# A seven-product output projection in another block order, and a seam issued from one table of steps

## The chip, the cores and the metric

The program runs on one core of one Trainium2 chip. The metric is the device time of one execution in microseconds (us). The core has TensorE (PE, matrix products into PSUM), VectorE (DVE), ScalarE (ACT), GpSimd (POOL) and SyncE (SP, whose queue issues most DMAs). Each engine works through its own queue in order; semaphores tie the queues together.

## The reference, cut to what matters

One layer of a hybrid decoder on 1024 rows of width 1024 in float32. Two attention mixers are gated, added and projected; then comes a gated feed-forward block of inner width 2816 (`D_FF`).

```python
y = jax.nn.sigmoid(g_a) * (o_a @ w_o_swa[l]) + jax.nn.sigmoid(g_b) * (o_b @ w_o_mla[l])
x = x + y @ w_out[l]
h = rmsnorm(x, ffn_norm_g[l])
x = x + (jax.nn.silu(h @ w_gate[l]) * (h @ w_up[l])) @ w_down[l]
return rmsnorm(x, final_norm_g)
```

## The kernel before, in words

**Precision.** A float32 operand is used as a high and a low part. `split(hi, lo, src)` (L160, L161) lets ACT round the source into `hi`, and VectorE, or another engine if named, forms `lo = src - hi`. `mm3` (L167 to L169) multiplies with three matmuls: high by high, high by low, low by high.

**Seven products.** The large matrix products are cut into 2 x 2 blocks and formed from seven block products in place of eight, at the price of sums of blocks. Block products are numbered q = 1 to 7. Products 1, 2, 5 and 3 accumulate in PSUM bank group "A" (product 5 starts a new accumulation) and 6, 7 and 4 in group "B". `class Seven` does this for the gates and for the feed-forward: for each pair j of weight column blocks and each matrix m (gate "g", up "u"), `mix` forms sums of weight blocks on GpSimd, `prep` splits the weights of the next product, and `run` issues its 12 matmuls and what takes its result. Before product q = 7 `prep` also corrects one weight block on GpSimd (L172, `wr<-wr,sm`). In a raw weight tile the two column blocks of a pair lie in turn, so one block is four runs of 128 elements.

**Output projection.** x + y @ w_out runs as seven products of four row tiles t each, in the order `X_ORDER = (1, 2, 6, 7, 5, 4, 3)`. One step (q, t) is 12 matmuls into a PSUM tile `xo`; `xo_done` then adds or subtracts that tile on VectorE in one to three half rows of x2, the eight row tiles of the new x. Row tiles 0 to 3 are complete with the sixth product (q = 4), row tiles 4 to 7 with the seventh (q = 3). A list `prep` of 30 splits of y and w_out is worked off between the steps.

**The seam.** Each complete row tile b goes through `row_sum` (sum of squares on ACT, two small GpSimd operations), `row_norm` (one VectorE operation giving `xn`, and the store of x2 to DRAM), eight 128x128 transposes on TensorE into two PSUM tiles `tp` (`to_ps`), and `to_h`. For b below 4 `to_h` splits them as blocks b11 and b21 and keeps a copy `hraw`. For b from 4 it forms the block sums: t2 and t3 with b22 at once, t1 and t4 from what remains in `hraw`, split last by `late_split`. GpSimd does three subtractions per row tile there: `hraw - t`, the low part of t3 and the low part of t4. Feed-forward product 1 needs b11, 2 needs b21, 6 needs t2, 7 needs t3, 5 needs t1, 4 needs t4 and 3 needs b22. The feed-forward starts with products 1 and 2 of pairs 0 and 1 (`head`), eight runs that need row tiles 0 to 3 only, and then does 6, 7, 5, 4, 3 of pair 0, and of pair 1.

**Order.** Between `in_order.__enter__()` and its exit the queues of PE, DVE, ACT and POOL hold the instructions in the order in which the program issues them; elsewhere a planner orders them. Before, this stretch begins with the sixth product. After it, `ffn.run` prepares four runs ahead. `act_out` and `wd_out` prepare the operands of the down projection for each pair j: `wd_out` loads two tiles of w_down, subtracts blocks on GpSimd four times and stores the tiles to `rb_d`. It stands at q = 5 of pairs 0 and 1 and at q = 2 of the later ones; that of the last pair stands at q = 4 of pair 3.

**Buffers.** Tiles of 4 KB per partition come from 21 slots (`U`), tiles of 8 KB from 17 slots (`V`), PSUM tiles from two groups of four banks (`P1`, `PX`).

## Time and profile before

| | |
|---|---|
| median of 3 runs | 1364.37 us (1363.83 to 1364.56) |
| the profiled execution's own time | 1360.19 us |
| its span, first to last instruction | 1358.4 us |
| PE busy / weight loads busy | 1331.8 us / 1112.0 us |
| DVE / ACT / POOL busy | 944.6 / 653.4 / 596.2 us |
| granted TensorE clock | 0.999 |

Rows of groups read: line, engine, operation, out<-in, shapes, count, then busy time in all, mean ns of one, and idle time before them with what ended it. Rows of windows read: stretch, length, busy time and count of PE, weight loads, DVE, ACT, POOL (engines without work left out), then granted clock, DMA share and GB/s. Rows of waits read: who waited, on whom, us in total, times, longest. A busy PE is not PE at its peak, so counts of matmuls per window tell more than its busy time.

### The profile page before, as it was taken

Reading aid. Unit: us, or ns where it says so; the run is one execution under the profiler, and the core shown is the slowest. Engines: PE = TensorE matmul, PEld = TensorE weight load, DVE = VectorE, ACT = ScalarE, POOL = GpSimd, SP = SyncE. Lnnn points to the kernel's source line nnn. Section 1 sums busy time; section 2 is a strip of 40 time slices with the busy share of each in tenths; the row PEclk is TensorE's granted clock in tenths of the full one; section 3 lists DMA queues with packets and bytes.
Section 4 is the critical chain, followed back from the end, with each engine's and each line's share of the span. In section 5 each row is a group of like instructions: output and inputs, shape, how many; then the busy total and the mean of one; then the engine's idle time right before and its main releaser. Section 6 shows DMA issues by size and latency. Waiting matters only on the chain.

```text
span 1358.4 us, 18967 instructions
## 1 busy us (share of the span) xinstructions
PE 1331.8 (98%) x6552; PEld 1112.0 (82%) x6552; DVE 944.6 (70%) x1527; ACT 653.4 (48%) x1317; POOL 596.2 (44%) x636
## 2 busy tenths in 40 slices
PE   9999999999999999999999999999999999999997
PEld 6899878878788888888887788888888888888886
DVE  6868767776777887489878866666656664664862
ACT  7433667665567777654357232322332332644452
POOL 1115545553066555131045875766665541022521
PEclk9999999999999999999999999999999999999999
DMA  9454332335100111598041353645444425996503
GB/s 360 161 182 154 115 106 82 98 121 174 71 2 13 43 32 32 219 307 264 31 171 62 112 188 140 227 178 178 147 153 165 163 85 184 379 385 237 171 16 140
DMA packets 78239, 205.39 MB, mean 151 GB/s; under 512 B 8768, under 2 KB 15424, under 8 KB 77504
## 3 DMA queue, kind: packets, MB, share of 16 engines
q1 hardware_dynamic: 76848, 199.99, 41.5%
...
## 4 chain that ended last, share of the span: by engine, by line
PE 72%; DVE 7%; ACT 4%; issue 3%; POOL 3%; DMA 0%; POOLq 0%; ACTq 0%; DVEq 0%
PE fa L169 7%; PE fa L167 7%; PE fa L168 7%; PE fd L168 5%; PE fd L167 5%; PE fd L169 5%; PE fb L167 5%; PE fb L169 5%; PE fb L168 5%; DVE wl L161 2%; PE pTb L1161 2%; PE xo L167 1%; PE xo L168 1%; PE xo L169 1%; PE oA L167 1%
## 5 line engine op out<-in xcount | busy, mean ns | idle before, releaser
L161 DVE TENSOR_TENSOR wl<-wr,wl 128x512 fp32r<-128x512 f32 x150 | 154.6, 1052 | 75.4 <-ACT wl L160 75.1
L161 DVE TENSOR_TENSOR lrv<-lr,lrv 128x1024 fp32r<-128x1024 f32 x77 | 105.0, 1396 | 49.7 <-ACT lrv L160 47.1
L160 ACT CAST lrv<-lr 128x1024 fp32r<-128x1024 f32 x77 | 80.1, 1052 | 96.3 <-PE fd L169 56.0
L169 PE MATMUL fd<-lrv 128*128 128x512 f32 x308 | 119.9, 389 | 0.0
L168 PE MATMUL fd<-lrv 128*128 128x512 f32 x308 | 119.9, 389 | 0.0
L167 PE MATMUL fd<-lrv 128*128 128x512 f32 x308 | 119.9, 389 | 0.0
L172 POOL TENSOR_TENSOR wr<-wr,sm 128x512 f32<-128x512 f32 (+1 forms) x38 | 46.8, 1241 | 121.2 <-DVE wl L161 115.1
L160 ACT CAST wl<-wr 128x512 fp32r<-128x512 f32 x150 | 87.3, 623 | 3.1 <-DVE wr L816 2.6
L161 DVE TENSOR_TENSOR wl<-sm,wl 128x512 fp32r<-128x512 f32 x60 | 55.2, 946 | 45.4 <-ACT wl L160 45.4
L295 POOL TENSOR_SCALAR ms<-ss 128x1 f32<-128x1 f32 x32 | 9.8, 305 | 140.4 <-ACT xn L1582 62.5
L1146 POOL TENSOR_TENSOR denb<-denb,neg_one 128x1 f32<-128x1 f32 x64 | 36.4, 570 | 75.0 <-ACT p L1145 64.3
L167 PEld LDWEIGHTS fd<-lrv 128*128 128x128 f32 x308 | 57.8, 188 | 12.1
L169 PEld LDWEIGHTS fd<-lrv 128*128 128x128 f32 x308 | 57.8, 188 | 12.0
L168 PEld LDWEIGHTS fd<-lrv 128*128 128x128 f32 x308 | 57.8, 188 | 11.9
L1145 ACT ACTIVATE p<-scb,nmb 128x384 f32<-128x384 f32 (+3 forms) x64 | 47.5, 743 | 36.8 <-DVE nmb L1144 35.0
L161 DVE TENSOR_TENSOR ptl<-pTb,pth 128x512 fp32r<-128x512 f32 (+2 forms) x96 | 50.0, 549 | 13.6 <-ACT pth L160 12.8
L1144 DVE CUSTOM_DVE_ANT_0 scb<-scb,mask 128x384 f32<-128x384 f32 (+3 forms) x64 | 48.5, 758 | 14.1 <-PE scb L1136 13.7
L1485 ACT ACTIVATE act<-sm 128x512 f32<-128x512 f32 x11 | 7.0, 633 | 103.7 <-DVE sm L175 103.7
L1147 POOL TENSOR_SCALAR p<-p,denb 128x384 f32<-128x384 f32 (+3 forms) x64 | 49.1, 768 | 6.3
L1485 ACT ACTIVATE act<-pu 128x512 f32<-128x512 f32 x22 | 13.9, 632 | 74.8 <-DVE pu L175 74.8
L160 ACT CAST pth<-pTb 128x512 fp32r<-128x512 f32 (+2 forms) x96 | 42.9, 482 | 13.5 <-PE pTb L1161 12.9
L169 PE MATMUL fa<-t1h,wl 128*128 128x512 f32 x120 | 46.8, 391 | 2.6 <-DVE wl L161 2.6
...
## 6 DMA issues: line engine op xcount, KB each, us to landing
...
wr<-in_w_gate_dram SPq DMA_DIRECT2D x22, 512.0 KB, 4.3
wr<-in_w_up_dram SPq DMA_DIRECT2D x22, 512.0 KB, 5.0
wd<-in_w_down_dram SPq DMA_DIRECT2D x22, 512.0 KB, 6.4
rb_d<-wd SPq DMA_DIRECT2D x22, 512.0 KB, 2.6
la_d<-sd SPq DMA_DIRECT2D x22, 512.0 KB, 4.8
...
```

Source lines behind the costliest of these rows:

```text
L160: nc.scalar.copy(hi, src)
L161: (eng or nc.vector).tensor_tensor(lo, src, hi.bitcast(F32), op=ALU.subtract)
L167: nc.tensor.matmul(ps, ah, bh, start=first and i == 0, stop=False, skip_group_check=go_on)
L168: nc.tensor.matmul(ps, ah, bl, start=False, stop=False, skip_group_check=go_on)
L169: nc.tensor.matmul(ps, al, bh, start=False, stop=last and i == n - 1, skip_group_check=go_on)
L172: eng.tensor_tensor(out, a, b, op=ALU.subtract)
L1144: nc.vector.tensor_tensor_reduce(s_, s_, m_, 1.0, -NEG, op0=ALU.add, op1=ALU.min, accum_out=nm)
L1145: nc.scalar.activation(p_, s_, AF.Exp, scale=-1.0, bias=nm, accum_out=den)
L1146: nc.gpsimd.tensor_tensor(den, den, neg_one[:, 0:1], op=ALU.pow)
L1147: nc.gpsimd.tensor_scalar(p[:, 0:w], p[:, 0:w], den, 0.0, op0=ALU.mult, op1=ALU.add)
L1161: nc.tensor.transpose(pp[:, i], p[:, blk(k0 + i)], ident)
L1485: nc.scalar.activation(dst, src, AF.Silu)
```

## The change

- The output projection runs in the order (1, 2, 6, 5, 3, 7, 4), and the two halves of the rows change roles in it (`y_split`, `y_sums`, `xo_done`). Row tiles 0 to 3 are now complete with the fifth product (q = 3), row tiles 4 to 7 with the seventh (q = 4). Bank group "A" comes from `PX` and "B" from `P1`, the reverse of before.
- The stretch in program order begins with the fifth product, and everything in it is issued from the string `SEAM`, one token for a step: `x` an output projection step, `y` a split from `prep`, `s` and `n` row sum and norm, `T` transposes, `h`, `c` splits and copy of a row tile below 4, `a b 0 2 l 3 i e g F H` single operations of a row tile from 4, `t` and `v` the splits of t1 and t4, `m` and `M` the weight sums of pairs 0 and 1, `p` one prepared weight, `f` one feed-forward product, `D` the new DMA sums.
- The subtractions `i`, `H` and the low part of `v`, which GpSimd did, stand on VectorE. Signs are turned in several places (`plus`, scale -1).
- For pair 0 the correction before q = 7 is left out of `prep`; two accumulating DMAs issued by GpSimd (`mix_sum`, step 2) do it.
- `wd_out` of pairs 0 and 1 moves to q = 5 of pairs 2 and 3.
- A raw weight tile holds each column block of a pair in one run of 512 elements.
- `mix_load` and the other steps of `mix_sum` are defined and not called.

```diff
+                op = add if self.plus else sub
                 for k in range(0, 4, n):
                     k = slice(k, k + n)
                     add(s[:, 0, k], a21[:, k], a22[:, k], eng_)
-                    sub(s[:, 1, k], s[:, 0, k], a11[:, k], eng_)
-                    sub(a21[:, k], a11[:, k], a21[:, k], eng_)
+                    op(s[:, 1, k], s[:, 0, k], a11[:, k], eng_)
+                    op(a21[:, k], a11[:, k], a21[:, k], eng_)
...
+        def mix_sum(self, j, step):
+
+            def plus(dst, src):
+                nc.gpsimd.dma_start(dst, src, accum_op=ALU.add)
+
+            for m in self.ms:
+                a11, a22 = self.src[m][j, 0][:, 0], self.src[m][j, 1][:, 1]
+                s = self.sums[(j, m)]
+                if step == 0:
+                    for i in range(2):
+                        plus(s[:, i], a22)
+                elif step == 1:
+                    plus(s[:, 1], a11)
+                    plus(self.part(j, m, 0, 1), a11)
+                else:
+                    plus(self.part(j, m, 1, 0), s[:, 1])
...
-            if q == 7:
+            if q == 7 and j not in self.by_dma:
                 a12, s1 = self.part(j, m, 1, 0), self.sums[(j, m)][:, 1]
                 for k in range(0, 4, self.piece):
                     k = slice(k, k + self.piece)
-                    sub(a12[:, k], a12[:, k], s1[:, k], nc.gpsimd)
+                    (add if self.plus else sub)(a12[:, k], a12[:, k], s1[:, k], nc.gpsimd)
...
-                add(u2, ps, p1, nc.vector)
+                add(u2, ps, p1, nc.vector) if not self.plus else sub(u2, p1, ps, nc.vector)
             elif q == 7:
-                add(u3, ps, p1, nc.vector)
+                (sub if self.plus else add)(u3, ps, p1, nc.vector)
...
-        t = U("wr", F32, (P, 4, 2, P))
+        t = U("wr", F32, (P, 2, 4, P))
...
         if j == 0:
-            nc.vector.tensor_scalar(t[:, k], t[:, k], g, None, op0=ALU.mult)
+            nc.vector.tensor_scalar(t[:, :, k], t[:, :, k], g, None, op0=ALU.mult)
         else:
-            nc.scalar.activation(t[:, k], t[:, k], AF.Copy, scale=g)
+            nc.scalar.activation(t[:, :, k], t[:, :, k], AF.Copy, scale=g)
...
-        for sh in (1, 0):
...
-        src = y_new[0][:, k] if q == 5 else y[k + 4 * (q in (2, 3, 4))][:, half({1: 1, 2: 1, 6: 1, 7: 0, 4: 0, 3: 1}[q])]
+        src = y_new[0][:, k] if q == 5 else y[k + 4 * (q in (2, 3, 4))][:, half({1: 0, 2: 0, 6: 0, 7: 1, 4: 1, 3: 0}[q])]
...
-        a21, a11, a22, a12 = y[k][:, half(0)], y[k][:, half(1)], y[4 + k][:, half(0)], y[4 + k][:, half(1)]
+        a21, a11, a22, a12 = y[k][:, half(1)], y[k][:, half(0)], y[4 + k][:, half(1)], y[4 + k][:, half(0)]
...
-    def to_h(pss, b):
+    tps = {}
+
+    def seam_step(what, b):
 
         c = b % 4
-        if b < 4:
-            if b == 0:
-                new_h("b11")
-                new_h("b21")
-            raw1[b] = U("hraw", F32, (P, 2, 4, P))
+        pss = tps.get(b)
+        if what == "T":
+            tps[b] = to_ps(xn_of.pop(b))
+            if b in (0, 4):
+                for name in ("b11", "b21") if b == 0 else ("b22", "t2", "t3"):
+                    new_h(name)
+        elif what == "h":
             for kh in range(2):
                 split_h(("b11", "b21")[kh], c, pss[kh])
+        elif what == "c":
+            raw1[c] = U("hraw", F32, (P, 2, 4, P))
             for kh in range(2):
-                nc.scalar.copy(raw1[b][:, kh], pss[kh])
-            return
-        if b == 4:
-            for name in ("b22", "t2", "t3"):
+                nc.scalar.copy(raw1[c][:, kh], pss[kh])
+        elif what == "a":
+            t23[c] = U("t23", F32, (P, 2, 4, P))
+            nc.scalar.copy(t23[c][:, 1], pss[0])
+        elif what == "b":
+            nc.scalar.copy(hq["b22"][0][:, :, blk(c)], pss[1])
+        elif what == "0":
+            sub(raw1[c][:, 0], raw1[c][:, 0], pss[0], nc.vector)
+        elif what == "2":
+            nc.vector.scalar_tensor_tensor(t23[c][:, 0], pss[1], -1.0, raw1[c][:, 0], op0=ALU.mult, op1=ALU.subtract)
+        elif what == "l":
+            sub(hq["b22"][1][:, :, blk(c)], pss[1], hq["b22"][0][:, :, blk(c)].bitcast(F32), nc.vector)
+        elif what == "3":
+            sub(t23[c][:, 1], t23[c][:, 1], pss[1], nc.vector)
+        elif what == "i":
+            add(raw1[c][:, 1], raw1[c][:, 1], t23[c][:, 0], nc.vector)
+        elif what == "e":
+            nc.scalar.activation(hq["t2"][0][:, :, blk(c)], t23[c][:, 0], AF.Copy, scale=-1.0)
+        elif what == "g":
+            nc.vector.scalar_tensor_tensor(hq["t2"][1][:, :, blk(c)], t23[c][:, 0], -1.0,
+                                           hq["t2"][0][:, :, blk(c)].bitcast(F32), op0=ALU.mult, op1=ALU.subtract)
+        elif what == "F":
+            nc.scalar.copy(hq["t3"][0][:, :, blk(c)], t23[c][:, 1])
+        elif what == "H":
+            sub(hq["t3"][1][:, :, blk(c)], t23[c][:, 1], hq["t3"][0][:, :, blk(c)].bitcast(F32), nc.vector)
+        elif what in "tv":
+            name = "t1" if what == "t" else "t4"
+            if name not in hq:
                 new_h(name)
-        r = raw1.pop(c)
-        t23 = U("t23", F32, (P, 2, 4, P))
-        nc.scalar.copy(t23[:, 1], pss[0])
-        sub(r[:, 0], pss[0], r[:, 0], nc.vector)
-        sub(t23[:, 0], pss[1], r[:, 0], nc.vector)
-        nc.scalar.copy(hq["t2"][0][:, :, blk(c)], t23[:, 0])
-        sub(r[:, 1], r[:, 1], t23[:, 0], nc.gpsimd)
-        late.append((c, r))
-
-        def rest():
-            sub(t23[:, 1], pss[1], t23[:, 1], nc.vector)
-            nc.scalar.copy(hq["b22"][0][:, :, blk(c)], pss[1])
-            nc.scalar.copy(hq["t3"][0][:, :, blk(c)], t23[:, 1])
-            for name, src, eng in (("t2", t23[:, 0], nc.vector), ("b22", pss[1], nc.vector),
-                                   ("t3", t23[:, 1], nc.gpsimd)):
-                hi, lo = hq[name]
-                sub(lo[:, :, blk(c)], src, hi[:, :, blk(c)].bitcast(F32), eng)
-
-        return rest
-
+            split_h(name, c, raw1[c][:, what == "v"], (nc.vector, nc.vector)[what == "v"])
+            done_of[c] = done_of.get(c, 0) + 1
+            if done_of[c] == 2:
+                raw1.pop(c)
...
     def load_w(j, kh):
         if j == 0:
-            t = [U("wr", F32, (P, 4, 2, P)) for _ in range(2)]
+            t = [U("wr", F32, (P, 2, 4, P)) for _ in range(2)]
         else:
-            v = V("wr", F32, (P, 2, 4, 2, P))
+            v = V("wr", F32, (P, 2, 2, 4, P))
...
-            add(other, ps, other, nc.vector)
+            if (f, sh) == (1, 1):
+                sub(other, other, ps, nc.vector)
+            else:
+                (add if sh else sub)(other, ps, other, nc.vector)
...
-                {(1, 6): [("load", 2, 0)], (1, 7): [("load", 2, 1)], (1, 5): [("mix", 2)]})
+                {(1, 6): [("load", 2, 0)], (1, 7): [("load", 2, 1)], (1, 5): [("mix", 2)]}, plus=True, src={"g": w_gate, "u": w_up},
+                by_dma=(0,))
...
-    def late_split(c):
-        r = late[c][1]
-        for i, name in ((0, "t1"), (1, "t4")):
-            if c == 0:
-                new_h(name)
-            split_h(name, c, r[:, i], (nc.vector, nc.gpsimd)[i])
-        late[c] = None
...
-    X_ORDER = (1, 2, 6, 7, 5, 4, 3)
-    xns = []
-    rests = []
+    X_ORDER = (1, 2, 6, 5, 3, 7, 4)
 
     def xo_done(q, t):
         ps = bank["A" if q in (1, 2, 5, 3) else "B"][t]
-        for b, d, sign in {1: ((t, 0, 0), (t, 1, 0), (4 + t, 1, 1)), 2: ((4 + t, 0, 1),), 6: ((4 + t, 1, 0),), 7: ((t, 1, 1),),
-                           5: ((t, 1, 0),), 4: ((t, 0, 1),), 3: ((4 + t, 1, 1),)}[q]:
+        for b, d, sign in {1: ((4 + t, 0, 0), (4 + t, 1, 0), (t, 1, 1)), 2: ((t, 0, 1),), 6: ((t, 1, 0),), 7: ((4 + t, 1, 1),),
+                           5: ((4 + t, 1, 0),), 4: ((4 + t, 0, 1),), 3: ((t, 1, 1),)}[q]:
...
-    PREP = {(4, 0): 1, (4, 1): 2, (3, 0): 3, (3, 1): 4}
+
+    def xo_step(q, t):
+        if t == 0:
+            if q in (1, 6, 5):
+                key = "A" if q in (1, 5) else "B"
+                bank[key] = [(PX if key == "A" else P1)("xo") for _ in range(4)]
+            xo_ops[q] = (*yl.pop(q), *wl.pop(q))
+        ah, al, bh, bl = xo_ops[q]
+        mm3(bank["A" if q in (1, 2, 5, 3) else "B"][t],
+            [((ah[:, k, blk(t)], al[:, k, blk(t)]), (bh[:, k], bl[:, k])) for k in range(4)],
+            first=q in (1, 6, 5), go_on=q in (2, 7, 4, 3))
+        if t == 3:
+            del ah, al, bh, bl, xo_ops[q]
+        xo_done(q, t)
+
+    xo_ops = {}
...
-    for q in X_ORDER:
-        if q == 4:
-            in_order.__enter__()
-        if q in (1, 6, 5):
-            key = "A" if q in (1, 5) else "B"
-            bank[key] = [(P1 if key == "A" else PX)("xo") for _ in range(4)]
-        (ah, al), (bh, bl) = yl.pop(q), wl.pop(q)
...
-            if (q, t) == (5, 1):
-                ffn.load_part(0, 1)
-            if q == 3 and t < 2:
-                ffn.load_part(1, t)
-            mm3(bank["A" if q in (1, 2, 5, 3) else "B"][t],
-                [((ah[:, k, blk(t)], al[:, k, blk(t)]), (bh[:, k], bl[:, k])) for k in range(4)],
-                first=q in (1, 6, 5), go_on=q in (2, 7, 4, 3))
-            xo_done(q, t)
-            n_x += 0.4 if q == 1 else 1.8
+            xo_step(q, t)
+            n_x += 0.4 if q == 1 else 1.9
...
-            r = {4: 0, 3: 4}.get(q)
-            if r is not None:
-                if q == 3:
-                    next_h()
-                row_sum(r + t)
-                if r + t >= 1:
-                    row_norm(r + t - 1)
-                if r + t in (1, 3):
-                    ffn.mix(0, None, "gu"[r + t == 3])
-                if (q, t) == (4, 2):
-                    next_h()
-            if (q, t) in PREP:
-                ffn.prep_to(PREP[q, t])
+    in_order.__enter__()
+    ffn.load_part(0, 1)
     ffn.n_ahead = 1
-    ffn.run()
-    row_norm(7)
-    ffn.prep_to(5)
-    ffn.run()
-    ffn.prep_to(6)
-    next_h()
-    rests.pop(0)()
-    ffn.run()
-    rests.pop(0)()
-    ffn.prep_to(7)
-    ffn.run()
-    ffn.prep_to(8)
-    next_h(ffn.run)
-    rests.pop(0)()
-    ffn.prep_to(9)
-    ffn.run()
-    next_h()
-    ffn.run()
-    rests.pop(0)()
-    ffn.prep_to(10)
-    ffn.run()
-    for i in range(1, 5):
-        late_split(i - 1)
-        if i == 2:
-            ffn.prep_to(11)
-        if i == 3:
-            ffn.prep_to(12)
-        ffn.run()
-    ffn.prep_to(14)
-    ffn.mix(1)
+    SEAM = ("y x30 y s0 n0 x31 y x32 s1 n1 s2 x33 y s3 T0 n2 h0 x70 y m0 c0 T1 n3 x71 h1 c1 T2 x72 h2 c2 m1 "
+            "T3 x73 h3 p c3 x40 s4 p p x41 n4 s5 x42 s6 n5 x43 s7 n6 T4 p a4 34 b4 f 04 24 l4 i4 n7 p e4 f F4 "
+            "g4 H4 T5 a5 05 b5 25 l5 35 i5 p f e5 g5 p T6 a6 F5 b6 06 l6 f 26 36 i6 H5 e6 g6 F6 f p T7 H6 p f "
+            "a7 37 07 b7 27 l7 i7 e7 g7 F7 p D H7 f f t0 p f v2 t1 v1 v0 f p t2 p f t3 p v3 p f p M")
+    for s_ in SEAM.split():
+        what, args = s_[0], [int(n) for n in s_[1:]]
+        if what == "x":
+            if args[0] == 4 and args[1] < 2:
+                ffn.load_part(1, args[1])
+            xo_step(*args)
+        elif what == "y":
+            f, *rest = prep.pop(0)
+            f(*rest)
+        elif what == "s":
+            row_sum(*args)
+        elif what == "n":
+            row_norm(*args)
+        elif what == "m":
+            ffn.mix(0, None, "gu"[args[0]])
+        elif what == "D":
+            ffn.mix_sum(0, 2)
+        elif what == "M":
+            ffn.mix(1)
+        elif what == "p":
+            ffn.prep_to(ffn.n_prep + 1)
+        elif what == "f":
+            ffn.run()
+        else:
+            seam_step(what, *args)
     in_order.__exit__(None, None, None)
     ffn.n_ahead = 4
 
     while ffn.n_run < len(ffn.seq):
         j, q, m = ffn.run()
-        if (q, m) == (5 if j < 2 else 2, "u"):
-            if j < HF - 1:
-                wd_out(j)
+        if (q, m) == (2, "u") and 2 <= j < HF - 1:
+            wd_out(j)
+        if (q, m) == (5, "u") and j in (2, 3):
+            wd_out(j - 2)
         if (j, q, m) == (3, 4, "u"):
             wd_out(HF - 1)
         if (q, m) == (7, "g") and j > 0:
...
-        return m.reshape(2, 4, P, 2, n, P).transpose(4, 0, 2, 1, 3, 5)
+        return m.reshape(2, 4, P, 2, n, P).transpose(4, 0, 2, 3, 1, 5)
```

27 lines of the change are left out of this document (14 added, 13 removed).

## The prediction

> **What bounds the kernel now.** I read the page first, then the busy time by 20 us windows, then the waits of one stretch, then that stretch's groups on VectorE and GpSimd, then single instructions. Page and windows:
>
> ```profile
> PE 1331.8 (98%) x6552; PEld 1112.0 (82%) x6552; DVE 944.6 (70%) x1527; ACT 653.4 (48%) x1317; POOL 596.2 (44%) x636
> ```
> ```profile
> 700.00:720.00 20.00, 19.95 (x104) 16.43 (x103) 15.53 (x21) 14.61 (x29) 11.30 (x14) 1.00 0.45 175
> 720.00:740.00 20.00, 18.15 (x86) 14.36 (x85) 18.67 (x25) 13.65 (x25) 9.00 (x7) 1.00 0.04 14
> 740.00:760.00 20.00, 15.76 (x67) 12.08 (x66) 18.24 (x17) 7.30 (x15) 19.66 (x14) 1.00 0.36 119
> 760.00:780.00 20.00, 19.76 (x88) 16.06 (x87) 17.90 (x21) 6.37 (x12) 14.13 (x10) 1.00 0.36 131
> 780.00:800.00 20.00, 20.00 (x90) 16.57 (x89) 14.43 (x17) 5.01 (x9) 15.78 (x11) 1.00 0.63 222
> 900.00:940.00 40.00, 40.00 (x178) 33.10 (x178) 24.07 (x30) 12.73 (x24) 25.17 (x19) 1.00 0.43 152
> ```
>
> The columns are length, then busy time and count of PE, weight loads, DVE, ACT and POOL, the granted clock, DMA share and GB/s. TensorE is the bound: 178 matmuls in 40 us, one per 0.2247 us, with no idle. So only stretches with fewer matmuls can be shortened, and one of them is the seam, 700 to 780. It also holds transposes:
>
> ```profile
> 700.00:720.00 20.00, 4.16 (x33) 3.74 (x32) 5.22 (x8) 7.08 (x14) 1.00 0.45 175
> 720.00:740.00 20.00, 2.08 (x16) 1.87 (x16) 9.22 (x14) 3.97 (x7) 1.00 0.04 14
> ```
> ```profile
> 702.38 0.39 PE L169 MATMUL xo<-woh,yl 128*128 128x512 f32 x1
> 702.61 1.03 PE L1424 MATMUL tp<-ident,xn 128*128 128x128 f32 x8
> 703.40 0.48 PE L167 MATMUL xo<-woh,yh 128*128 128x512 f32 x1
> 703.72 0.40 PE L168 MATMUL xo<-wol,yh 128*128 128x512 f32 x1
> ```
>
> A set of 8 transposes costs 703.72 - 702.61 = 1.11 less one matmul, 0.89 us. By weight loads (the first pair of rows above counts those of the transposes), the four windows hold 71, 69, 66 and 87 matmuls and 4, 2, 0 and 0 sets: 19.5, 17.3, 14.8 and 19.5 us of work in 20. **8.8 us are lost**, the most this seam can give. Who made TensorE wait, from 676 to 790:
>
> ```profile
> PE fa L169 <- DVE wl L161: 2.6, 1, 2.6
> PE fb L169 <- DVE wl L161: 1.6, 2, 1.2
> PE fa L167 <- ACT pu L793: 1.1, 1, 1.1
> PE fb L168 <- DVE t2l L172: 0.8, 1, 0.8
> DVE wl L161 <- ACT wl L160: 6.9, 8, 1.7
> ```
>
> TensorE's four rows make 6.1 of the 8.8; the rest is draining and restarting at each stop. The waits end on VectorE (or on ACT, in whose queue the waited-for copy stands). Its groups from 711 to 766, GpSimd's, and both windows:
>
> ```profile
> L161 DVE TENSOR_TENSOR wl<-wr,wl 128x512 fp32r<-128x512 f32 x10 | 13.4, 1355 | 1.6 <-ACT wl L160 1.6
> L161 DVE TENSOR_TENSOR wl<-sm,wl 128x512 fp32r<-128x512 f32 x5 | 6.6, 1332 | 0.2 <-ACT wl L160 0.2
> L161 DVE TENSOR_TENSOR t1l<-hraw,t1h 128x512 fp32r<-128x512 f32 x4 | 4.7, 1177 | 0.0
> L1587 DVE SCALAR_TENSOR_TENSOR xn<-x,rstd,ffng 128x1024 f32<-128x1024 f32 x3 | 3.8, 1278 | 2.1 <-POOL rstd L298 2.1
> L172 DVE TENSOR_TENSOR t<-tp,hraw 128x512 f32<-128x512 f32 x4 | 2.8, 692 | 0.3
> ```
> ```profile
> L172 POOL TENSOR_TENSOR wr<-wr,sm 128x512 f32<-128x512 f32 x4 | 6.9, 1736 | 0.0
> L161 POOL TENSOR_TENSOR t4l<-hraw,t4h 128x512 fp32r<-128x512 f32 x4 | 6.6, 1664 | 0.3 <-ACT t4h L160 0.3
> L172 POOL TENSOR_TENSOR hraw<-hraw,t 128x512 f32<-128x512 f32 x4 | 6.1, 1528 | 10.4 <-DVE t L172 10.4
> L172 POOL TENSOR_TENSOR t3l<-t,t3h 128x512 fp32r<-128x512 f32 x4 | 5.2, 1297 | 3.3 <-ACT t3h L1456 2.9 <-PE tp L1424 0.4
> ```
> ```profile
> 676.00:711.00 35.00, 35.00 (x176) 29.23 (x174) 25.63 (x35) 16.24 (x30) 15.55 (x18) 1.00 0.41 151
> 711.00:766.00 55.00, 48.86 (x219) 38.67 (x219) 48.84 (x55) 30.71 (x57) 38.30 (x28) 1.00 0.19 68
> ```
>
> VectorE is busy 48.8 of 55 us, but a subtraction with both inputs in SBUF takes 1.2 to 1.4 us while GpSimd works, against 0.69 with one input in PSUM (the row from tp). With GpSimd silent (771 us), the chain shows the true pace, 0.60 per operation, for the same splits:
>
> ```profile
> 770.87 0.60 DVE pu L175
> 771.47 0.60 DVE wl L161
> 772.07 0.60 DVE act L1487
> ```
>
> **The change part by part.** *Product order (1, 2, 6, 5, 3, 7, 4) with the row halves exchanged.* The same 336 matmuls and the same number of adds. Rows 0 to 3 of x are whole after the fifth product instead of the sixth, so their sums, norms, transposes and splits may lie under two products. From the start of the fifth to the end of the seventh, TensorE has 3 x 48 x 0.2247 + 4 x 0.89 = 36.0 us. VectorE's list there: 12 adds, 8 splits of T0 to T3, 3 y splits and 3 gate or up splits (26 at 0.60), six norms and two w splits (8 at 1.28): 25.8 us. It is covered, as 25.6 of 35 was before. Without cover each operation would cost 0.60. The sums of pair 0 (m0, m1) stay on GpSimd, now wholly beneath these products.
>
> *GpSimd work moved.* Three subtractions per block, 12 in all (hraw, t3l, t4l: 17.9 us in the rows), go to VectorE, at 0.60 each 7.2 us. The two q = 7 corrections of pair 0 go to two accumulating DMAs, and both weight-down preparations of pairs 0 and 1 leave the seam. So from the transposes of row 4 to the first product on t2 GpSimd holds row statistics and two DMA issues, no 128x512 work.
>
> *The stretch that decides*: from the last output product to the ninth feed-forward product, the first on t2. TensorE has four transpose sets and eight products of 12 matmuls: 3.6 + 21.6 = 25.1 us. VectorE must by then have done: the last add, seven operations for each of blocks 4 to 7 (3, 0, 2, l, i, g, H) less the last H, six weight splits, one product of up and gate: 1 + 27 + 6 + 1 = 35 at 0.60 = 21.0, two norms 2.6, and about 0.4 until the last add can start: 24.0. Nothing is lost at 0.60; if each took 0.68, its length when alone, 26.8, so 1.7 lost, and near 3 with restarts at two stops (0.3 each) and ACT's copies queued between. The chain behind T7 (0.9 transposes, 0.6 copy, five operations, 0.6 cast, 0.6 split: 5.7 with its hand-overs) lies under three products, 8.1. ACT was busy 30.7 of 55. I take 1.6 left, of 0 to 3: the rows in a full queue are the 0.60 ones, but the list alternates between two engines. **Seam: 8.8 - 1.6 = 7.2 us less.**
>
> Then t1 and t4: 8 split operations beside 4 accumulations and 6 weight splits, 18 x 0.60 = 10.8 us beside four products, 10.8: just covered, and the last weight splits are wanted later. The pair-1 sums (M) come on GpSimd after that, six products before their first use (16 us against 6 x 1.7).
>
> *Layout of the weight pairs* (four runs of 128 become one of 512). Strided and whole splits, GpSimd quiet:
>
> ```profile
> L161 DVE TENSOR_TENSOR wl<-wr,wl x35: 679/693/1247, 165.1 to 346.2; 128x512 fp32r<-128x512 f32 x35
> 771.39 0.68 DVE L161 TENSOR_TENSOR wl<-sm,wl 128x512 fp32r<-128x512 f32 x1
> ```
>
> 0.69 against 0.68: nothing, in the gates as here. The gate scalings now read two runs instead of one; also nothing, under matmuls.
>
> *The DMA sums* (D). POOL's earlier accumulating DMAs:
>
> ```profile
> wo<-wo POOLq DMA_DIRECT2D x6, 512.0 KB, 10.0
> ```
>
> About 10 us to land; they are wanted by the split for q = 3, prepared after the list, more than 13 us behind their place. Covered; uncovered, up to 10 us. GpSimd's and SP's queues behind them hold nothing that needs them.
>
> *Weight-down preparation of pairs 0 and 1 moved to pairs 2 and 3*: each four GpSimd operations and four DMAs on SP.
>
> ```profile
> L172 POOL TENSOR_TENSOR wd<-wd 128x512 f32<-128x512 f32 x20 | 30.2, 1510 | 9.2 <-DMA wd<-in_w_down_dram 8.9
> L172 POOL TENSOR_TENSOR wd<-wd,wd 128x512 f32<-128x512 f32 x20 | 27.4, 1370 | 0.9 <-DMA wd<-in_w_down_dram 0.7
> ```
>
> A pair lasts 168 x 0.2247 = 37.7 us, in which GpSimd has 25.2/40 of it, 23.7; plus 2 x (1.51 + 1.37) = 5.8 gives 29.5; pair 3, where the last pair's preparation stands too, 35.3. It fits, the second time narrowly, and pair 4 has 14 us free for what spills. The stores to rb_d wait on SP for GpSimd, and the next pair's weight loads queue behind them; the nearest load stands nine products (24 us) later. Nothing, or some 2 us in pair 3 if that fails. The stores of x rows and the weight loads keep their number.
>
> In the Trainium skill, SBUF — State Buffer, section "Who interferes with whom" says that a VectorE operation with two SBUF inputs and a GpSimd operation that reads SBUF hold the shared port pair exclusively, so that the later one waits for the whole of the other. By that rule a collision costs a whole GpSimd operation, 1.3 us (t3l), where the rows show 1.36 - 0.60 = 0.76. Emptying GpSimd then saves more VectorE time; TensorE's 8.8 stays the ceiling. The same page's section "SBUF: two separate sides" speaks against D: a DMA from GpSimd can starve for descriptors while VectorE runs a two-port copy. No such copy stands in the list, and no run here shows it.
>
> **The rivals.**
> A. *VectorE starves between ACT's halves.* Before, it idled 6.9 us for wl casts. In the new stretch only 1.1 us are spare; if the 6.9 come back, 5.8 are lost plus 0.3, and the gain is 2.7: 1361.7 us. For it: seven operations a block alternate with four of ACT's. Against: weight casts stand several steps ahead.
> B. *Slower: GpSimd's pair-0 sums slip into the stretch.* Place: m0 and m1, and D's issue, beside blocks 4 to 7. Seventeen operations there (4 i, 4 g, 3 H, 6 splits) have both inputs in SBUF; at 0.76 more each 12.9 us, of which 1.1 is spare: 11.8 lost against 8.8, 1367.4 us. It decides from (8.8 + 1.1)/0.76 = 13 of the 17 on. Against: six operations of 1.7 last 10 us, and their inputs load earlier. By the rule above, at 1.3 each, 21 lost: 1376.6 us.
> C. *The seam's gain does not show*: the same stops return elsewhere, because a block's tile must wait for a buffer (21 of 4 KB, and I count 20 to 21 in use at T4). If ACT stands there 1.8 us for each of four blocks, 7.2 return: 1364.4 us. For it: the count; against: x rows come free as their norms end.
>
> **How the numbers follow.** The profiled execution took 1360.19 us around its span of 1358.4; the median shown is 1364.37, 4.18 more, and I carry that difference along: 1353.0 for a profiled execution, **1357.2** for the median. Chances: forecast (3 to 8.8 less) 0.74, A 0.10, B 0.07, C 0.09. The forecast's own range is 1355.6 to 1361.4; to leave out no more than 2 in 10 it reaches to A on one side and a little below the ceiling on the other, for small gains in the pairs that now have less GpSimd work: 1354.8 to 1362.5. A difference within 0.2% (2.7 us) could not be told from no change: faster 0.80 (forecast and half of A), same 0.13, slower 0.07.
>
> **What would show it.** Right: windows from the sixth product to the first 20 us of pair 1 at 89 weight loads (transposes aside); no 128x512 operation of GpSimd between T4 and the ninth product; splits there at 0.60 to 0.69; waits of TensorE of 2 us or less. Wrong: splits at 1.2 or more there (B); VectorE idle behind ACT (A); ACT or VectorE waiting for a DMA or a norm before t23 (C); matmul rates below 178 per 40 us in pairs 2 and 3 (weight-down).

## The result, and the profile after

The changed kernel took 1353.31 us (median of 4 runs, 1352.32 to 1353.75). The kernel before, run beside it, lay at 1361.94 to 1364.56, and the ratio is **0.994, with a 95% interval of 0.9924 to 0.9956**: 8.2 us less, of 6.0 to 10.4. The prediction said 1357.2, from 1354.8 to 1362.5: its sign was right, and the time fell 1.5 us below its range. Taken by the ratio from the 1364.37 that the prediction started from, the changed kernel stands at 1356.2.

The profiled execution of the changed kernel took 1353.75 us, with a span of 1352.0. Its page and its windows over the seam, with one earlier window:

```profile
PE 1328.2 (98%) x6552; PEld 1111.1 (82%) x6552; DVE 942.4 (70%) x1539; ACT 654.2 (48%) x1317; POOL 575.5 (43%) x624
```
```profile
600.00:620.00 20.00, 18.04 (x80) 14.59 (x80) 18.33 (x24) 4.77 (x6) 3.62 (x3) 1.00 0.72 231
...
700.00:720.00 20.00, 20.00 (x98) 16.73 (x97) 16.28 (x23) 13.07 (x25) 5.02 (x10) 1.00 0.41 132
720.00:740.00 20.00, 20.00 (x98) 16.72 (x97) 19.61 (x33) 14.70 (x28) 0.00 (x0) 1.00 0.10 33
740.00:760.00 20.00, 18.42 (x82) 14.93 (x81) 18.73 (x20) 7.14 (x15) 13.27 (x8) 1.00 0.13 48
760.00:780.00 20.00, 20.00 (x90) 16.57 (x89) 12.66 (x20) 3.72 (x8) 12.03 (x9) 1.00 0.34 131
```

TensorE is without a gap in 700 to 740, where the transposes of the later row tiles now stand with the first feed-forward products. GpSimd ran nothing in 720 to 740 (9.0 us before). In 740 to 760 there are 81 matmuls, 8 below the full 89; before there were 66. And a window that was full before, 600 to 620, now holds 80. Who made TensorE wait, in the seam (676 to 790) and around 600 us:

```profile
PE fa L168 <- DVE t1l L161: 1.6, 1, 1.6
```
```profile
PE oB L169 <- DVE wl L161: 2.0, 1, 2.0
```

Of the stops of before (6.1 us in four rows) one is left, at the t1 product, where the longest of before stood too:

```profile
755.90 0.50 PE L169 MATMUL fa<-t1h,wl 128*128 128x512 f32 x1 [2.61 <-DVE wl L161]
```

A measure that the rest of the kernel can't blur is the time from the first matmul of the output projection (`xo`) to the first of the down projection (`fd`). The kernel before, then the changed one:

```profile
630.06 0.39 PE L167 MATMUL xo<-woh,yh 128*128 128x512 f32 x1
...
1141.22 0.39 PE L167 MATMUL fd<-lrv 128*128 128x512 f32 x1
```
```profile
631.08 0.39 PE L167 MATMUL xo<-woh,yh 128*128 128x512 f32 x1
...
1135.26 0.39 PE L167 MATMUL fd<-lrv 128*128 128x512 f32 x1
```

511.2 us against 504.2: **7.0 us less**, where the prediction took 7.2 from the seam. This stretch is called the xo-fd stretch below, read from the same two rows in every kernel. (The expectations call its end "the first classifier matmul"; it is that of the down projection. They give 511.1 for the kernel before, whose rows above give 511.16.)

### The profile page after: what moved, and what is told of

The parts are those of the page before. It is cut to its first block, busy times and chain, and to the rows that moved or that the text cites. A ratio compares the mean times of both kernels' runs of the same rounds, so it can differ in the third digit from the quotient of the medians.

```text
span 1352.0 us, 18958 instructions
## 1 busy us (share of the span) xinstructions
PE 1328.2 (98%) x6552; PEld 1111.1 (82%) x6552; DVE 942.4 (70%) x1539; ACT 654.2 (48%) x1317; POOL 575.5 (43%) x624
## 4 chain that ended last, share of the span: by engine, by line
PE 78%; DVE 5%; issue 2%; POOL 2%; ACT 2%; POOLq 0%; ACTq 0%; DVEq 0%
PE fa L169 7%; PE fa L168 7%; PE fa L167 7%; PE fb L169 5%; PE fb L167 5%; PE fb L168 5%; PE fd L168 5%; PE fd L167 5%; PE fd L169 5%; PE pTb L1189 2%; PE xo L167 2%; PE xo L168 2%; PE xo L169 2%; PE ob L1212 1%; PE ob L1211 1%
## 5 line engine op out<-in xcount | busy, mean ns | idle before, releaser
L161 DVE TENSOR_TENSOR wl<-wr,wl 128x512 fp32r<-128x512 f32 x150 | 147.7, 1006 | 73.3 <-ACT wl L160 73.0
L175 POOL TENSOR_TENSOR wr<-wr,sm 128x512 f32<-128x512 f32 x20 | 30.6, 1530 | 99.4 <-DVE wl L161 99.4
L1173 ACT ACTIVATE p<-scb,nmb 128x384 f32<-128x384 f32 (+3 forms) x64 | 47.6, 745 | 35.9 <-DVE nmb L1172 34.2
L175 POOL TENSOR_TENSOR sm<-wr,wr 128x512 f32<-128x512 f32 (+1 forms) x36 | 40.2, 1123 | 32.2 <-PE fb L169 26.2
L168 PE MATMUL fa<-t1l,wl 128*128 128x512 f32 x120 | 46.8, 390 | 1.6 <-DVE t1l L161 1.6
```

The source lines that it names most:

```text
L161: (eng or nc.vector).tensor_tensor(lo, src, hi.bitcast(F32), op=ALU.subtract)
L168: nc.tensor.matmul(ps, ah, bl, start=False, stop=False, skip_group_check=go_on)
L175: eng.tensor_tensor(out, a, b, op=ALU.add)
L1173: nc.scalar.activation(p_, s_, AF.Exp, scale=-1.0, bias=nm, accum_out=den)
```

## The experiments

The two theories at the start: **port** (GpSimd's 128x512 work slows VectorE's operations with two SBUF inputs; taking it away is the gain) and **order** (row tiles that are whole one product earlier give VectorE the time; the new product order is the gain). The stretches are those of the profiled executions, one or two for each kernel; the medians were taken in several sittings, so kernels are compared by their ratios to the kernel before.

| kernel | xo-fd stretch, us | rows of TensorE's waits over 0.2 us in 676 to 790 | median, us | ratio to before (95%) |
|---|---|---|---|---|
| before | 511.2 | 2.6, 1.6, 1.1, 0.8 | 1364.1 | 1 |
| before, again | 511.2 | 2.6, 1.6, 1.1, 0.8 | 1361.92 | 0.9999 (0.9987 to 1.0011) |
| changed | 504.2 | 1.6 | 1353.31 | 0.994 (0.9924 to 0.9956) |
| changed, again | 504.2 | 1.6 | 1354.12 | 0.9946 (0.9928 to 0.9964) |
| all GpSimd work back | 508.3 | 2.4, 1.8, 0.6 | 1357.65 | 0.9971 (0.9958 to 0.9983) |
| later row tiles | 508.5 | 1.8, 1.6, 0.4 | 1358.18 | 0.9975 (0.9962 to 0.9987) |
| before with light GpSimd | 516.4 | 4.7, 3.2 | 1363.92 | 1.0018 (1.0007 to 1.0028) |
| subtractions back | 510.4 | 3.5, 0.6, 0.6 | 1360.70 | 0.9986 (0.9975 to 0.9997) |
| subtractions and corrections back | 506.0 | 1.8, 0.6, 0.3 | 1356.91 | 0.9962 (0.9949 to 0.9975) |
| spare weight rows back | 504.6 | 1.6 | 1354.57 | 0.9941 (0.9926 to 0.9957) |
| corrections back | 504.2 | 1.6 | 1354.76 | 0.9942 (0.9929 to 0.9954) |
| t1 first | 506.8 | 2.8 | 1355.78 | 0.9958 (0.994 to 0.9975) |
| pair-1 sums on VectorE | 502.3 | none | 1351.81 | 0.9924 (0.9912 to 0.9937) |
| the same, and mix on VectorE | 502.3 | none | **1349.11** | **0.9907 (0.9894 to 0.992)** |

### Both kernels again

No edit: the kernel before and the changed kernel, against further runs of the kernel before.

> The kernel before, unchanged, for a second profile and as a measure of what no change looks like. The first profile of before took 1360.2 us while its other runs took 1361.9 to 1364.6. Theory collision: a 128x1024 multiplication of GpSimd (sg<-ar,sg) in the last part of the gating stage, near 600 us, sometimes hits the low split of the w_o weights on VectorE; where it does, TensorE stands about 2 us there, as it does in the profile of the changed kernel, and the time is 2 to 4 us longer. Then this profile shows such a stop if it is nearer 1364, and none if nearer 1360. Rival: the spread lies elsewhere (loads from HBM at the start, the end), and the stretch from 560 to 640 us has no stop in either case. Ratio 1.000 within 0.002.

> The changed kernel, unchanged, on the chip of the comparisons that follow. All theories: ratio 0.992 to 0.996 (5 to 10 us less); TensorE's stops between the first output product and the end of pair 0 about 2 us in all, the one stop at the split of t1 with GpSimd at work.

The kernel before ranged from 1358.6 to 1365.18 us over 29 runs (median 1362.77), so the three runs in the prediction stood in its upper part. Its second profile has the same seam and the same stretch (511.2), but TensorE waits elsewhere, 2.3 us at 602 us, where the first profile shows no wait. The second profile of the changed kernel has the reverse: no wait there, where its first has 2.0. VectorE and GpSimd at that place, in the kernel before run again, then in the changed kernel run again:

```profile
598.83 3.40 DVE L161 TENSOR_TENSOR wl<-wr,wh 128x1024 fp32r<-128x1024 f32 x1
...
598.38 2.76 POOL L1304 TENSOR_TENSOR sg<-ar,sg 128x1024 f32<-128x1024 f32 x1 [1.36 <-ACT sg L1217]
```
```profile
600.10 1.21 DVE L161 TENSOR_TENSOR wl<-wr,wh 128x1024 fp32r<-128x1024 f32 x1
...
600.83 2.76 POOL L1332 TENSOR_TENSOR sg<-ar,sg 128x1024 f32<-128x1024 f32 x1 [1.20 <-ACT sg L1245]
```

Where GpSimd's multiplication starts first, the split takes 3.40 us and the product that needs it waits; where the split starts first, it takes 1.21 and nothing waits. The two are less than 1 us apart, so either kernel falls now on one side, now on the other.

The expectation failed in one point: it tied the wait to executions nearer 1364 us, and this one, with the wait, took 1360.78. The wait is only one part of the scatter. In the 14 profiles of this document, whatever the kernel, the same matmul (the 2901st, of the scores `scb`) starts anywhere between 528.0 and 531.7 us; from there to the output projection it is 98.6 us in the five profiles without the wait and 100.8 to 102.6 in the nine with it. The gain therefore can't be read from one total, and the xo-fd stretch, which begins behind this place, is read instead.

### The two halves of the change

All GpSimd work of the seam back, in the changed kernel:

```diff
-             add(raw1[c][:, 1], raw1[c][:, 1], t23[c][:, 0], nc.vector)
+             add(raw1[c][:, 1], raw1[c][:, 1], t23[c][:, 0], nc.gpsimd)
...
-             sub(hq["t3"][1]..., nc.vector)
+             sub(hq["t3"][1]..., nc.gpsimd)
...
-             split_h(name, c, raw1[c][:, what == "v"], (nc.vector, nc.vector)[what == "v"])
+             split_h(name, c, raw1[c][:, what == "v"], (nc.vector, nc.gpsimd)[what == "v"])
...
-                 by_dma=(0,))
+                 by_dma=())
...
-             "... F7 p D H7 f f t0 ..."
+             "... F7 p H7 f f t0 ..."
...
-         if (q, m) == (2, "u") and 2 <= j < HF - 1:
-             wd_out(j)
-         if (q, m) == (5, "u") and j in (2, 3):
-             wd_out(j - 2)
+         if (q, m) == (5 if j < 2 else 2, "u"):
+             if j < HF - 1:
+                 wd_out(j)
```

> The changed kernel with all of the GpSimd work put back: the three subtractions per row tile on GpSimd, the corrections before q = 7 of pair 0 on GpSimd and no accumulating DMAs, weight-down preparation of pairs 0 and 1 at its old place. Product order and step table stay. Theory port (the gain is VectorE time won by an idle GpSimd): VectorE's SBUF splits in the seam are at 1.2 to 1.4 us again, TensorE loses 6 to 9 us there, ratio 0.998 to 1.001. Rival order (the gain is that row tiles 0 to 3 are complete one product earlier): 0.994 to 0.996, as without this edit.

And the row tiles whole one product later, with a table of steps written for it by hand:

```diff
-     X_ORDER = (1, 2, 6, 5, 3, 7, 4)
+     X_ORDER = (1, 2, 6, 7, 5, 3, 4)
...
-             if (q, t) == (5, 0):
+             if (q, t) == (7, 0):
...
-     SEAM = ("y x30 y s0 n0 x31 y x32 s1 n1 s2 x33 y s3 T0 n2 h0 x70 y m0 c0 T1 n3 x71 h1 c1 T2 x72 h2 c2 m1 "
-             "T3 x73 h3 p c3 x40 s4 p p x41 n4 s5 x42 s6 n5 x43 s7 n6 T4 ...
+     SEAM = ("y x50 y x51 y x52 y x53 y x30 s0 n0 x31 x32 s1 n1 s2 x33 s3 T0 n2 h0 x40 m0 c0 T1 n3 x41 s4 h1 c1 T2 x42 n4 s5 h2 c2 m1 "
+             "T3 x43 s6 n5 h3 p c3 p p s7 n6 T4 ...
```

> The changed kernel with the product order (1, 2, 6, 7, 5, 3, 4): row tiles 0 to 3 are complete with the sixth product, as in the kernel before, tiles 4 to 7 with the seventh; the table's steps for tiles 0 to 3 move one product later, all else stays. Theory port: VectorE has about 19 us of work under the two products and four transposes that remain (25 us), so nothing is lost, ratio 0.993 to 0.996 and TensorE's seam stops stay near 2 us. Rival order: the stops come back, 5 us or more, ratio 0.998 or above.

The second of the three hunks only keeps the loads of pair 0 at the fourth product.

Neither theory holds alone. Measured on the stretch, the first gives back 4.2 of the 7.0 us and the second 4.3: together more than there is. So the other side was tried too, GpSimd's relief in the kernel before, without the new product order and without the table of steps (the corrections before q = 7 stay on GpSimd):

```diff
-         sub(r[:, 1], r[:, 1], t23[:, 0], nc.gpsimd)
+         sub(r[:, 1], r[:, 1], t23[:, 0], nc.vector)
...
-                                    ("t3", t23[:, 1], nc.gpsimd)):
+                                    ("t3", t23[:, 1], nc.vector)):
...
-             split_h(name, c, r[:, i], (nc.vector, nc.gpsimd)[i])
+             split_h(name, c, r[:, i], (nc.vector, nc.vector)[i])
...
-         if (q, m) == (5 if j < 2 else 2, "u"):
-             if j < HF - 1:
-                 wd_out(j)
+         if (q, m) == (2, "u") and 2 <= j < HF - 1:
+             wd_out(j)
+         if (q, m) == (5, "u") and j in (2, 3):
+             wd_out(j - 2)
```

> The kernel before, with its order of products, its planner and its corrections, and two things of the change: the three subtractions per row tile on VectorE, and the spare weight rows' work at pairs 2 and 3. Stretch from first output product to first classifier matmul: 511.1 us in the kernel before, 504.2 in the changed one. Theory A (both halves are needed: the 12 operations of VectorE need the time that earlier row tiles give): 507 to 509.5, TensorE still waiting for VectorE in the seam, total about 1359. Theory B (the subtractions on GpSimd are the whole price, wherever the rows stand): 504.2 to 506, total about 1355.5. Theory C (VectorE with 12 more operations and no earlier start is later than before): over 511.1.

Theory C, the one against the change, holds: 516.4 us, **5.2 longer than before**. This is the slowest of the twelve executions (1367.12 us); by the ratio of all of them the kernel is 2.5 us slower than before (1.0 to 3.8). TensorE's waits, and ACT's and VectorE's rows ahead of the 2.9 us on `pu`:

```profile
PE fb L169 <- DVE wl L161: 4.7, 2, 2.7
PE fa L167 <- ACT pu L793: 3.2, 2, 2.9
```
```profile
735.47 0.62 ACT L1449 CAST t2h<-t 128x512 fp32r<-128x512 f32 x1 [2.02 <-DVE t L172]
...
738.32 0.59 ACT L793 COPY pu<-fa 128x512 f32<-128x512 f32 x1
...
733.96 0.68 DVE L172 TENSOR_TENSOR hraw<-tp,hraw 128x512 f32<-128x512 f32 x1
734.75 0.69 DVE L172 TENSOR_TENSOR t<-tp,hraw 128x512 f32<-128x512 f32 x1
```

VectorE keeps its pace there (no operation that starts between 725 and 747 us is slowed), yet the row tile's chain passes through it and ACT in turn; ACT waits 2.02 us for the sum `t`, and the copy of a finished accumulation, for which TensorE waits, stands behind it in ACT's queue. The larger 4.7 us are something else. GpSimd, relieved, starts the sums of pair 1 at 746.67, beside VectorE's splits, and the weight splits that TensorE waits for take 1.75 us:

```profile
751.49 1.75 DVE L161 TENSOR_TENSOR wl<-wr,wl 128x512 fp32r<-128x512 f32 x1
...
750.98 1.71 POOL L175 TENSOR_TENSOR sm<-wr,wr 128x512 f32<-128x512 f32 x1
```

Behind two of these stops TensorE's granted clock falls to half, and matmuls start 0.43 us apart, which by my estimate from the 25 matmuls behind each stop costs 4.3 us, most of the 5.2 (the kernel before has none of it in its seam):

```profile
740.00:745.00 5.00, 5.00 (x14) 3.90 (x13) 4.81 (x9) 3.84 (x8) 0.00 (x0) 0.52 0.00 0
```

So the relief of GpSimd is a loss in the kernel before, the new order of products and steps is a gain with the old load (-2.8, all GpSimd work back against before), and both together give 7.0. **The new order of issue is what lets VectorE take the work over.** Which part of it, the product order or the table of steps, is told in part by the kernel with later row tiles. It has the light GpSimd and the table, but its row tiles 0 to 3 are whole with the sixth product, as in the kernel before, and it is 2.6 us shorter than before. What it loses against the changed kernel stands at one place, the first feed-forward product, which waits 1.8 us for ACT's cast of a weight and 0.35 for VectorE's, and then runs at 0.43 us a matmul:

```profile
714.09 0.50 PE L167 MATMUL fa<-b11h,wl 128*128 128x512 f32 x1 [1.81 <-ACT wl L160]
```

From there on TensorE waits as in the changed kernel, 1.6 us at the t1 product and nowhere else up to 790 us. So the earlier row tiles aren't what the takeover needs most. Their worth beside a light GpSimd is at most 4.3 us, since the stop may belong to this hand-written table. The table with the old load and the old product order wasn't run, so what each part is worth by itself stays open.

### Which part of GpSimd's work

In the changed kernel, only the three subtractions per row tile back on GpSimd (the first three hunks of "all GpSimd work back"):

> The changed kernel with only its three subtractions per row tile back on GpSimd (four row tiles, 12 operations). Measured on the stretch from the first output product's matmul to the first classifier matmul: 504.2 us in both profiles of the changed kernel, 508.3 with all GpSimd work back (subtractions, q=7 corrections, spare weights), 511.1 and 511.2 in the kernel before. Theory A (each part of the GpSimd work costs the stop that stands beside it in that profile): the stops at the t2, t3 and t1 products come back, 0.9 + 0.5 + 0.2, so 505.6 to 506.0 and a total of about 1355.5. Theory B (the load on GpSimd counts as one backlog and the subtractions alone fit into its idle time): no new stop, 504.2 to 504.6. Theory C (the subtractions are the whole price): 507.5 to 508.5.

Only the spare weight rows back at pairs 0 and 1 (its last hunk):

> The changed kernel with only the spare weight rows' work (wd_out) of pairs 0 and 1 back beside pairs 0 and 1. Stretch from first output product to first classifier matmul, 504.2 us in the changed kernel. Theory A (each part costs its own stop): the stop of 2.1 us at the t3 product that stood at 774 us with all GpSimd work back returns, 506.3 to 506.7, total about 1356. Theory B (one backlog): without the other work ahead of it on GpSimd the spare rows' subtractions run earlier, beside operations that are not yet awaited, and the stretch is 504.2 to 505. Theory C (the subtractions are the whole price): 504.2 to 504.4.

Only the corrections before q = 7 back on GpSimd, without accumulating transfers (its fourth and fifth hunks):

> The changed kernel with only the q=7 corrections back on GpSimd (no accumulating transfers). Stretch from first output product to first classifier matmul, 504.2 us in the changed kernel. Theory A (each part costs its own stop): no stop of the profile with all GpSimd work back stands beside these corrections alone, so 504.2 to 505.0, total about 1354. Theory B (one backlog): 504.2 to 504.6. Rival D (the corrections push the first-use sums behind them, so that a product waits for GpSimd itself): 505.5 to 508, with a wait of TensorE that names GpSimd or a split of a sum.

The spare weight rows cost 0.4 us of stretch, as theory B had it, and the corrections nothing, as theories A and B both had it. So those two moves of the change gain next to nothing by themselves. The subtractions cost 6.2 us, more than all the work together (4.2): no theory had that. The place is one split of weights, on VectorE, with GpSimd's rows below it:

```profile
733.12 6.86 DVE L161 TENSOR_TENSOR wl<-sm,wl 128x512 fp32r<-128x512 f32 x1
```
```profile
732.59 1.84 POOL L761 DMA_DIRECT2D wr<-sm  x2
733.78 1.97 POOL L172 TENSOR_TENSOR t3l<-t,t3h 128x512 fp32r<-128x512 f32 x1
735.15 4.27 POOL L161 TENSOR_TENSOR t4l<-hraw,t4h 128x512 fp32r<-128x512 f32 x3
```

VectorE stood for 6.86 us over one operation that takes 0.68 elsewhere, while GpSimd ran four in a row, the last three at 1.42 each. TensorE waited 3.5 us and then ran eleven matmuls at 0.43 us, which by the same estimate is 2.5 of the 6.2; with all the work back none ran at that pace. The issue of the accumulating transfers stands just ahead. To tell whether it matters, subtractions and corrections were put back together (all hunks but the last), which removes the transfers and adds more GpSimd work:

> The changed kernel with the three subtractions per row tile and the q=7 corrections back on GpSimd (no accumulating transfers), the spare weight rows where the change has them. Stretch from first output product to first classifier matmul: 504.2 us in the changed kernel, 508.3 with all GpSimd work back, 510.4 with the subtractions alone back, where one VectorE split of weights lasted 6.86 us at 733.12, beside the issue of the accumulating transfers (732.59) and four GpSimd operations behind it. Theory T (issuing the accumulating transfers among GpSimd's operations is what starves VectorE): without them no split over 2 us, and the stops are those of the profile with all back without its 2.1 us stop at 774 us: 505.5 to 506.5. Theory S (a row of GpSimd operations is enough to starve VectorE, with or without transfers): again a split over 4 us and 508.5 to 511.

Theory T holds: 505.98 us, no split over 1.8, and by ratio 3.3 us below the kernel with the subtractions alone back (0.9962 against 0.9986). The kernel with all the work back, also without these transfers, has no split over 1.8 either. By these kernels the subtractions on GpSimd cost 1.8 us without the transfers and 6.2 with them, half clock included. Why VectorE gets no turn behind such an issue isn't settled: one profile shows when, not why.

### The stop that was left

In the changed kernel GpSimd's rows, VectorE's and TensorE's around the t1 product:

```profile
741.96 1.48 POOL L175 TENSOR_TENSOR sm<-wr,wr 128x512 f32<-128x512 f32 x1 [26.18 <-PE fb L169]
...
745.10 1.74 POOL L175 TENSOR_TENSOR wr<-wr 128x512 f32<-128x512 f32 x1
```
```profile
738.36 0.68 DVE L161 TENSOR_TENSOR wl<-wr,wl 128x512 fp32r<-128x512 f32 x1
...
740.39 0.69 DVE L161 TENSOR_TENSOR t1l<-hraw,t1h 128x512 fp32r<-128x512 f32 x1
...
742.80 1.20 DVE L161 TENSOR_TENSOR wl<-wr,wl 128x512 fp32r<-128x512 f32 x1
743.92 1.77 DVE L161 TENSOR_TENSOR t1l<-hraw,t1h 128x512 fp32r<-128x512 f32 x1
745.61 1.78 DVE L161 TENSOR_TENSOR wl<-sm,wl 128x512 fp32r<-128x512 f32 x1
747.31 0.68 DVE L172 TENSOR_TENSOR sm<-fb,pu 128x512 f32<-128x512 f32 x1
747.91 1.15 DVE L161 TENSOR_TENSOR t1l<-hraw,t1h 128x512 fp32r<-128x512 f32 x1
```
```profile
749.12 0.50 PE L168 MATMUL fa<-t1l,wl 128*128 128x512 f32 x1 [1.58 <-DVE t1l L161]
```

GpSimd starts the first-use sums of pair 1 at 741.96, released by a product of `fb` (by my reading, when their slot comes free). From then on the splits, with two inputs in SBUF, take up to 1.78 us instead of 0.69, while the additions with one input in PSUM (`sm<-fb,pu`) stay at 0.68. The last t1 split, at 747.91, is late by that. The first remedy was another order of the splits:

```diff
-             "... H7 f f t0 p f v2 t1 v1 v0 f p t2 p f t3 p v3 p f p M")
+             "... H7 f f t0 p f t1 t2 t3 f p p f v0 v1 v2 v3 p p f p f M")
```

> The changed kernel with the low halves of t1 taken ahead of those of t4 and of t2's and t3's splits of weights, and the order of the rest kept. Stretch from first output product to first classifier matmul, 504.2 us in the changed kernel, which has one stop there, 1.75 us longer than a matmul's pace at the t1 product (plus 0.1 to restart). My theory (VectorE is late at t1 because GpSimd's sums start beside its splits, and the order of the splits decides who meets them): the stop goes, the slowed splits are then those of t4, which have more time; 502.3 to 503.2, total about 1352.5. Rival (VectorE's whole backlog is what is late, in whatever order): the stop is only handed on to the t4 product or the one after, 503.8 to 504.4. Rival (the earlier t1 splits push the weight splits of the t2 and t3 products): over 504.4, with a stop at 735 to 745 us.

This expectation fell: 506.8 us, 2.6 more. Of its rivals the last has the size (over 504.4) but not the place: the stop stands at 750 us, not at 735 to 745. The t1 splits are out of the way at 738, as meant, but the four t4 splits behind them meet GpSimd, and the weight split that the t1 product also needs stands behind those:

```profile
741.87 6.36 DVE L161 TENSOR_TENSOR t4l<-hraw,t4h 128x512 fp32r<-128x512 f32 x4
748.15 1.75 DVE L161 TENSOR_TENSOR wl<-sm,wl 128x512 fp32r<-128x512 f32 x1
```

In both kernels VectorE is late because its splits meet GpSimd; the order only chooses who waits for it, and this one chose worse (2.83 us, and matmuls at 0.43 behind the stop). The second remedy takes the meeting away:

```diff
         elif what == "M":
-             ffn.mix(1)
+             ffn.mix(1, nc.vector)
```

> The changed kernel with one engine changed: the six first-use sums of pair 1, which stand last in the table, are made by VectorE instead of GpSimd. In the profile of the changed kernel GpSimd starts them at 741.96 us, nine VectorE splits beside them take 1.18 to 1.78 us instead of a pace of 0.60, and TensorE stops 1.75 us at the t1 product. My theory (VectorE is late at t1 because GpSimd's sums start beside its splits): without them the splits run at 0.60, the stop goes, and VectorE makes the sums after it, six times 0.60 = 3.6 us, before they are needed: stretch from first output product to first classifier matmul 502.2 to 502.8 instead of 504.2, no wait of TensorE over 0.5 us from 676 to 790, total about 1352. Rival (the t1 product is late by VectorE's own load): the stop stays, 503.8 to 504.4. Rival (3.6 us more on VectorE make the next products late): a new stop after 755 us, 504 to 506.

It came as expected: 502.31 us, with no wait of TensorE from 676 to 790. That is 8.85 us below the kernel before, which is the 8.8 that the prediction called the most this seam can give. (The expectation counts nine slowed splits in the changed kernel; there are eight, of 1.15 to 1.78.) The last t1 split now starts at 744.12, the six sums follow from 747.73, and the window that had 81 weight loads has 89:

```profile
744.12 0.68 DVE L161 TENSOR_TENSOR t1l<-hraw,t1h 128x512 fp32r<-128x512 f32 x1
...
747.73 0.68 DVE L175 TENSOR_TENSOR sm<-wr,wr 128x512 f32<-128x512 f32 x1
```
```profile
740.00:760.00 20.00, 20.00 (x90) 16.57 (x89) 19.97 (x31) 7.90 (x15) 3.14 (x2) 1.00 0.07 29
```

Six sums that take GpSimd 1.48 to 1.74 us each cost VectorE 0.60 each, but for one of 1.78 that meets a correction on GpSimd; leaving them on GpSimd cost VectorE more (eight slowed splits beside them and two corrections, each 0.5 to 1.1 us above the pace of 0.60).

### The collision near 600 us

On top of that, the four multiplications of the output mix on VectorE as well:

```diff
         if dc < 4:
-             nc.gpsimd.tensor_tensor(ga, ar.pop(dc), ga, op=ALU.mult)
+             nc.vector.tensor_tensor(ga, ar.pop(dc), ga, op=ALU.mult)
```

> The same, and the four multiplications of 128x1024 (sg by ar) of the output mix moved from GpSimd to VectorE. In four profiles of eight of changed and experimental kernels, and one of two of the kernel before, a split of 128x1024 on VectorE that starts just behind the last of these multiplications takes 3.40 us instead of 1.21 near 600 us, and TensorE waits 1.9 to 2.3 us; in the others it goes ahead of it and nothing waits. Theory (these collisions are most of the spread of 1351 to 1356 of the changed kernel): no wait of the oB products on VectorE, times closer together than 3 us, median 1350.5 to 1351.5. Rival (VectorE, busy 18.4 of 20 us there, can't take 1.2 us more four times): a wait of TensorE of 1 to 4 us between 585 and 625 us in the profile, median 1352 to 1355.

The theory holds, and its price was set too low: 1349.11 us, all four runs between 1348.92 and 1349.46, and no wait in 580 to 640. (The count in the expectation is one short: five of those eight profiles show the wait. Of the 13 profiles that have this multiplication on GpSimd, nine show it.) The window that held 80 weight loads is full although VectorE took four operations more:

```profile
600.00:620.00 20.00, 20.00 (x90) 16.55 (x89) 18.13 (x25) 4.23 (x6) 1.73 (x2) 1.00 0.74 230
```
```profile
596.92 1.21 DVE L1332 TENSOR_TENSOR sg<-ar,sg 128x1024 f32<-128x1024 f32 x1
...
599.89 1.22 DVE L161 TENSOR_TENSOR wl<-wr,wh 128x1024 fp32r<-128x1024 f32 x1
```

This version beats both kernels: by their ratios 12.7 us below the kernel before, and 4.5 to 5.3 below the changed one.

## Why the prediction was right, and where not

**The seam.** The prediction took 8.8 us as the most and 1.6 as left. Left are 1.97 from one start to the next at the t1 stop, less a matmul's pace, 1.75, and 0.1 of restart; 8.8 - 1.85 = 6.95, and the stretch shows 6.98. The total of this term was right by 0.2 us.

**The stretch that decides** (to the ninth feed-forward product) lost nothing, where 1.6 was taken. Its splits ran 0.60 apart with GpSimd silent, as the sum at that pace (24.0 in 25.1) had it, and the 0.68 that I feared as the pace did not come. So the 1.6 stood in the wrong place.

**The step that failed** is "just covered", with the sums of pair 1 coming on GpSimd "after that". It counted 18 operations at 0.60 against four products and let GpSimd begin when they were done. But the table orders each engine's queue, not one engine against another: GpSimd had been idle for 26 us, and began when a slot came free, amid the splits. Eight of them lost 0.5 to 1.1 us each, and the t1 product stopped. That the two errors are of one size is chance. The experiment with the sums on VectorE shows the cause: without them the stop is gone.

**GpSimd's work moved.** The price on VectorE (0.60 each) and the silence of GpSimd came as said. Not foreseen is that the parts don't add: +5.2 us for the relief without the new order of products and steps (+2.5 by all executions), -2.8 for that order alone, -7.0 together. The prediction costed the new order at "nothing lost" and gave it no share in the gain. Its 25.8 us are covered, as it said (its 36.0 us of TensorE are 35.9 by its own terms), but the third product isn't shown to be needed: with two, one stop of 1.8 us came back, and TensorE made no other wait that the changed kernel hasn't.

**The accumulating transfers and the spare weight rows** were put at nothing, and give nothing (0.0 and 0.4 us when undone). The transfers land in 3.7 us, not 10; they carry 256 KB each, half as much as those in the row that the prediction used:

```profile
wr<-sm POOLq DMA_DIRECT2D x2, 256.0 KB, 3.7
```

What was missed is the price that their issue may have beside GpSimd work (the 6.86 us above); in the changed kernel GpSimd is silent behind them.

**The layout** was put at nothing. It wasn't undone alone; a split of a weight block with GpSimd quiet takes 0.68 us in the changed kernel (the row at 738.36), and strided ones took 0.69.

**The rivals.** A, VectorE between ACT's halves, did not come in the changed kernel; its mechanism shows in the kernel before with light GpSimd, in the 2.9 us stop on ACT. B, sums of pair 0 in the stretch, did not come: GpSimd had nothing in 720 to 740. But its mechanism did come, with other sums and one stretch later: those of pair 1, beside eight splits. C, the stops back through buffers, did not come.

**The level.** The prediction subtracted 7.2 from a median of 1364.37. The 29 further runs of the kernel before have a median of 1362.77, and its spread is 6.6 us. By the profiles the collision near 600 us, with what follows it, makes 2.2 to 4.1 of that, and the time ahead of 532 us up to 3.7 more, whose cause stays open. No step of the prediction looked at either: they lie outside the change, and the profile of before had happened to miss the collision. By ratio the gain is 8.2 (6.0 to 10.4) and in the second set 7.4 (4.9 to 9.8); 7.0 lies in both.

**The price of a collision.** By the Trainium skill, SBUF — State Buffer, section "Who interferes with whom", the one that issues first holds the shared ports for its whole instruction and the other is blocked. I took that as a whole GpSimd operation, 1.3 us, against the row's 0.76. Here it cost 1.78 - 0.69 = 1.1 us at 128x512, and at 128x1024 3.40 - 1.21 = 2.2 against a GpSimd operation of 2.76, of which 2.3 were left when the split started. The trace agrees with the page, but the price is what is left of the other operation, not the whole of it. The rows of before that gave 0.76 were a mean over splits that met and splits that didn't.
